# A three-block transformer kernel: another order of work and of loads at the boundaries between its stages

## The chip, the core and the metric

The kernel runs on one core of one Trainium2 chip. A core has a matrix engine (TensorE, here PE; PEld is its loading of weights, which overlaps), a vector engine (VectorE, DVE), an activation engine (ScalarE, ACT), a general one (GpSimd, POOL) and a queue engine that here issues most transfers (SyncE, SP). Every engine works through its own instructions in order and waits for others by semaphores. The metric is the device time of one execution in microseconds (us); smaller is better.

## The reference

The reference is three blocks in a row over x of 512 tokens and 1024 features, all in fp32. Cut to what matters here:

```python
x = first_block(x, ...)    # x + gate1 * mixer(rms(x)), then x + gate2 * conv_ffn(rms(x)), then a last rms norm
x = second_block(x, ...)   # x + gate * (mixed(h) @ w_out), h = rms(x) * (1 + scale) + shift, then a last rms norm
x = third_block(x, ...):
    x = layer_norm(ALPHA * x + 0.5 * swiglu(x), ...)
    x = layer_norm(ALPHA * x + hybrid_mixer(x, mem, ...), ...)
    x = layer_norm(ALPHA * x + 0.5 * swiglu(x), ...)

def layer_norm(x, g, b):
    mu = mean(x); var = mean((x - mu) ** 2)
    return (x - mu) * rsqrt(var + eps) * g + b
```

Each stage thus ends in a product, a residual sum with the old x, and a norm over all 1024 features of a token, and the next stage begins with products of the normed result h. No product of the next stage can be complete before the norm's sum over all features is.

## The kernel before

Features lie on the partitions: x is 8 tiles of 128 features by 512 tokens, and so is h. A product in fp32 is made of three passes: each operand is split into a high part and the rest (`hi` and `lo`), and `dense` (L411) issues for every 128 by 128 weight tile `wh` x `a.hi` (L419), `wh` x `a.lo` (L420) and `wl` x `a.hi` (L422). All 8 (or 22) feature tiles k of the input are added up in one PSUM tile, called `mm` or `sd` after its pool; each pool has four.

Weights come as a stream of chunks of 8 such tiles (`Stream`, L71): a load of 512 KB by SP into one of two staging tiles `wst`, a cast to `whi` on ACT (L102), the rest `wlo` on DVE or POOL (L107). Six chunks have room; `_need` keeps three loaded ahead of the one in use. A chunk's room comes free when the last product with it is done.

`final_stage` (L442) is the end of every stage. The first `nfull` of the 8 output tiles m are made over all 512 tokens, the others in two halves of 256 tokens: first all remaining m of the first half, then all of the second. For every m, `epi` (in `residual`, L613) adds the old x, whose load POOL issues at that moment (L621), and `norm.push` adds to the norm's sums. `norm.finish` makes, for one half, a column sum on PE (L554: a product with a matrix of ones), a root on ACT (L228), a reciprocal on DVE (L229), and then h: per feature tile one `stt` (a scalar_tensor_tensor on DVE, L549), an ACT instruction that writes `hi`, and an `stt` that writes `lo`. It is a generator: the first half's h rows are emitted between the second half's products.

The layer norm (`NormLayer`, L332) subtracts a shift c, got from the first tile, from every x as it is pushed (L343, DVE), adds the x (L347) and their squares (L207), and in `finish` forms mean and variance (L352, L353, an `stt`) and subtracts the mean from 8 tiles, 5 of them on POOL (L357).

`dense_group` (L424) is the beginning of the next stage: a few products (jobs) are made in the first half, one job after the other, each through all 8 features, then all in the second half, with the same weights.

From the end of a first half's norm on, the next 4 chunks have their `wlo` made on POOL (`S.mark`, L485, and `held`), with an order that puts them behind the norm's root and reciprocal.

The program is written in this order, but a scheduler rearranges it for each engine by priorities and free buffers; what an engine then executes in what order is shown below.

The boundaries where this happens, with the numbers used in this document:

1. mixer `w_out` (L1012, rms norm) to `ffn_up` of the first block (L1064): jobs pg and pu for two m, pg in `mm`, pu in `sd`.
2. `w_down` (L1060, two rms norms at once) to `mlstm` of the second block: the gates `if2` (L1157), then q and k products in groups of two (L1231), convolutions over them (L1241), gates on 4 rows (L1159 and further), transposes of the gates (L1163), then v products and the scores (L495).
3. `w_out_2` (L1146, rms norm with a gain) to `ffn_up` of the third block.
4. swiglu's output (L1519, layer norm) to `dsa_index` (L1705): one product for the index keys, three for its queries, transposes of `iwT` (L1733).
5. `w_out_3` (L1547, layer norm) to `ffn_up` of the last swiglu.
6. the last swiglu's output, layer norm, and the kernel's end.

In 2, 4 and 6 the product has 22 feature tiles and `nfull` is 6; in the others it has 8, and `nfull` is 4.

## Time and profile before

| what | value |
|---|---|
| median of 3 runs | 3274.16 us (3274.14 to 3275.22) |
| the profiled execution | 3279.36 us |
| its span, first to last instruction | 3277.6 us |
| mean granted PE clock | 0.988 |
| PE idle in the span | 90 us |

The page's second part cuts the span in 40 slices. Two of its rows:

```profile
PE   8999999999999999999999999999899999989998
DVE  6997676588837756655787353333796747563334
```

Each digit is the busy share of a slice of 82 us in tenths (9 is 90% or more). DVE's row is read in the same way. PE drops below 9 in the first slice, in the slices of boundaries 4 and 5, and at the end; a wait of a few us at a boundary hardly shows at this grain, which is why the windows further down are 20 to 35 us wide. Rows of a timeline give start, length, engine, line, operation, names of output and inputs, form and count, and in brackets the idle time before, with what ended it. POOL's rows:

```profile
L107 POOL TENSOR_TENSOR wlo<-wst,whi 128x1024 fp32r<-128x1024 f32 x20 | 49.9, 2500 | 210.4 <-ACT whi L102 162.8 <-DVE t L549 39.7 <-DVE xh L549 3.6
L357 POOL TENSOR_TENSOR xh<-xh,t 128x256 f32<-128x256 f32 x30 | 26.4, 910 | 122.9 <-ACT t L352 111.8 <-PE sd L554 11.0
```

These are groups of instructions: busy time in all, mean ns of one, idle time before them. POOL made 20 splits (5 boundaries of 4) at 2.50 us each, and 30 subtractions of the mean.

### The profile page before, as it was taken

Reading aid. Unit: us, or ns where it says so; the run is one execution under the profiler, and the core shown is the slowest. Engines: PE = TensorE matmul, PEld = TensorE weight load, DVE = VectorE, ACT = ScalarE, POOL = GpSimd, SP = SyncE. Lnnn points to the kernel's source line nnn. Section 1 sums busy time; section 2 is a strip of 40 time slices with the busy share of each in tenths; the row PEclk is TensorE's granted clock in tenths of the full one; section 3 lists DMA queues with packets and bytes.
Section 4 is the critical chain, followed back from the end, with each engine's and each line's share of the span. In section 5 each row is a group of like instructions: output and inputs, shape, how many; then the busy total and the mean of one; then the engine's idle time right before and its main releaser. Section 6 shows DMA issues by size and latency. Waiting matters only on the chain.

```text
span 3277.6 us, 40053 instructions
## 1 busy us (share of the span) xinstructions
PE 3187.5 (97%) x15534; PEld 2639.8 (81%) x15534; DVE 2035.1 (62%) x3160; ACT 1310.2 (40%) x2010; POOL 193.6 (6%) x268
## 2 busy tenths in 40 slices
PE   8999999999999999999999999999899999989998
PEld 4778788888888888888887888888877787878887
DVE  6997676588837756655787353333796747563334
ACT  4665232344424444333665233222543535342222
POOL 2100000100001000000000010000200012020001
PEclk9999999999999999999999999999999999999999
DMA  5114776423333232222232333333323131333331
GB/s 204 52 58 134 238 223 199 140 90 97 106 113 105 78 90 84 84 90 85 74 97 74 110 116 103 103 106 106 117 75 124 61 105 61 122 103 97 106 109 62
DMA packets 123108, 352.52 MB, mean 108 GB/s; under 512 B 13978, under 2 KB 28668, under 8 KB 122788
## 3 DMA queue, kind: packets, MB, share of 16 engines
q1 hardware_dynamic: 118612, 336.18, 32.6%
q0 software_dynamic: 4304, 13.77, 1.3%
q8 instruction: 122, 2.00, 0.2%
q14 instruction: 70, 0.57, 0.1%
HBM read 337.27 MB, written 16.82 MB: 108 GB/s over the span
## 4 chain that ended last, share of the span: by engine, by line
PE 80%; DVE 11%; DMA 3%; issue 3%; ACT 2%; SPq 0%; POOL 0%; ACTq 0%; DVEq 0%; POOLq 0%
PE mm L420 19%; PE mm L419 19%; PE mm L422 18%; PE sd L420 4%; PE sd L422 4%; PE sd L419 4%; PE mm L440 2%; PE mm L439 2%; PE mm L438 2%; DVE wlo L107 2%; DMA gv<-in_wmod 2%; DVE xh L549 1%; PE sd L495 1%; PE sd L496 1%; PE sd L497 1%
## 5 line engine op out<-in xcount | busy, mean ns | idle before, releaser
L107 DVE TENSOR_TENSOR wlo<-wst,whi 128x1024 fp32r<-128x1024 f32 x496 | 609.4, 1230 | 614.7 <-ACT whi L102 605.5
L102 ACT CAST whi<-wst 128x1024 fp32r<-128x1024 f32 x485 | 509.1, 1051 | 1174.8 <-PE mm L420 732.5
L420 PE MATMUL mm<-xh,whi 128*128 128x512 f32 (+1 forms) x2256 | 857.5, 381 | 16.0 <-DVE xh L549 11.9
L419 PE MATMUL mm<-xh,whi 128*128 128x512 f32 (+1 forms) x2256 | 857.2, 381 | 14.5 <-ACT xh L364 10.5
L422 PE MATMUL mm<-xh,wlo 128*128 128x512 f32 (+1 forms) x2256 | 849.7, 379 | 0.0
L420 PEld LDWEIGHTS mm<-xh,whi 128*128 128x128 f32 x2256 | 430.4, 191 | 94.6 <-DVE xh L549 16.1
L419 PEld LDWEIGHTS mm<-xh,whi 128*128 128x128 f32 x2256 | 429.8, 191 | 94.5 <-ACT xh L364 11.4
L422 PEld LDWEIGHTS mm<-xh,wlo 128*128 128x128 f32 x2256 | 428.3, 191 | 74.0 <-issue 2.9
L419 PE MATMUL sd<-xh,whi 128*128 128x512 f32 (+1 forms) x576 | 215.2, 374 | 0.0
L420 PE MATMUL sd<-xh,whi 128*128 128x512 f32 (+1 forms) x576 | 214.6, 372 | 0.0
L422 PE MATMUL sd<-xh,wlo 128*128 128x512 f32 (+1 forms) x576 | 214.5, 372 | 0.0
L420 PE MATMUL mm<-d,whi 128*128 128x512 f32 (+1 forms) x540 | 187.7, 348 | 0.0
L422 PE MATMUL mm<-d,wlo 128*128 128x512 f32 (+1 forms) x540 | 187.2, 347 | 0.0
L419 PE MATMUL mm<-d,whi 128*128 128x512 f32 (+1 forms) x540 | 187.1, 347 | 0.0
L438 PE MATMUL mm<-whi,xh 128*128 128x512 f32 x336 | 131.7, 394 | 6.1 <-DVE whi L104 3.1
L439 PE MATMUL mm<-wlo,xh 128*128 128x512 f32 x336 | 132.8, 395 | 0.6 <-DVE wlo L107 0.6
L440 PE MATMUL mm<-whi,xh 128*128 128x512 f32 x336 | 132.0, 394 | 0.0
L549 DVE SCALAR_TENSOR_TENSOR t<-t,vec,t 128x441 f32<-128x441 f32 (+2 forms) x176 | 122.7, 701 | 9.6 <-ACT t L1046 5.3
L419 PEld LDWEIGHTS sd<-xh,whi 128*128 128x128 f32 x576 | 109.5, 190 | 18.8
L420 PEld LDWEIGHTS sd<-xh,whi 128*128 128x128 f32 x576 | 109.2, 190 | 18.8
L422 PEld LDWEIGHTS sd<-xh,wlo 128*128 128x128 f32 x576 | 109.2, 190 | 18.7
L1510 DVE TENSOR_TENSOR t<-t,sd 128x512 f32<-128x512 f32 x44 | 30.2, 688 | 144.7 <-PE sd L422 141.1
(482 smaller groups left out, 5187.6 us busy)
## 6 DMA issues: line engine op xcount, KB each, us to landing
wst<-in_w SPq DMA_DIRECT2D x516, 512.0 KB, 3.6
gv<-in_wmod SPq DMA_DIRECT2D x64, 256.0 KB, 3.5
gv<-in_wada SPq DMA_DIRECT2D x48, 256.0 KB, 3.5
t<-xd POOLq DMA_DIRECT2D x40, 256.0 KB, 3.6
xd<-xh SPq DMA_DIRECT2D x72, 128.0 KB, 1.8
wm<-in_wmod SPq DMA_DIRECT2D x32, 256.0 KB, 5.0
tmat<-trow SPq DMA_DIRECT2D x2, 2048.0 KB
tp<-tmat SPq DMA_DIRECT2D x16, 256.0 KB, 2.6
```

Source lines behind the costliest of these rows:

```text
L102: self.after(nc.scalar.copy(hi, st))
L107: self.after(eng.tensor_sub(lo, st, hi.bitcast(FT)))
L419: mm(ps, wh, a.hi[k], start=(k == 0), stop=False)
L420: mm(ps, wh, a.lo[k], start=False, stop=False)
L422: mm(ps, wl, a.hi[k], start=False, stop=(k == K - 1))
L438: mm(ps, a.hi[k][:, s], wh, start=(k == 0), stop=False)
L439: mm(ps, a.hi[k][:, s], wl, start=False, stop=False)
L440: mm(ps, a.lo[k][:, s], wh, start=False, stop=(k == K - 1))
L495: mm(ps, l[0], r[0], start=start, stop=False)
L496: mm(ps, l[0], r[1], start=False, stop=False)
L497: mm(ps, l[1], r[0], start=False, stop=stop)
L549: self.nc.vector.scalar_tensor_tensor(out, in0, s, in1, op0=op0, op1=op1)
```

## The change

It has six parts, all at the boundaries. (A) `dense_group` lets all its jobs step through the features together, and in the second half asks the stream to `fill` chunk rooms that came free; `final_stage` does so too. (B) The order marks and the splits on POOL are taken out: all `wlo` are on DVE. (C) The old x is loaded two tiles ahead, and in the layer norm POOL subtracts the shift from old x (not from tile 0) so that `push` doesn't. (D) In the layer norm's `finish` the square of the mean is made by ACT straight from the column sum, and all 8 subtractions of the mean are on DVE. (E) Two `sd` tiles are set aside ahead of the second half's norm (`spare`) and used by the next stage's first jobs. (F) In `mlstm` the gates' product and the first four q and k products are one group of five jobs, the gates come after it.

```diff
 class Stream:
-        self.after(eng.tensor_sub(lo, st, hi.bitcast(FT)))
-        self.held = max(self.held - 1, 0)
+        nc.vector.tensor_sub(lo, st, hi.bitcast(FT))
...
+    def fill(self, name, k, c0):
+        if not self.recording:
+            end = min(self.at[name, k, c0] + self.RING, (self.i - 1) // CH + 6, (len(self.order) + CH - 1) // CH)
+            while self.loaded < end:
+                self._load(self.loaded)
+                self.loaded += 1
...
 class NormLayer(Norm):
         if m == 0:
             nc.scalar.activation(self.named("c"), self.K.colsum(x), AF.Copy, scale=1.0 / P)
-        nc.vector.tensor_sub(x, x, self.named("c")[:, cols])
+            nc.vector.tensor_sub(x, x, self.named("c"))
...
-        nc.scalar.activation(mu, self.colsum("w", cols), AF.Copy, scale=1.0 / D)
-        nc.vector.tensor_mul(var, mu, mu)
+        sums = self.colsum("w", cols)
+        nc.scalar.activation(var, sums, AF.Square, scale=1.0 / D)
+        nc.scalar.activation(mu, sums, AF.Copy, scale=1.0 / D)
...
-            (nc.gpsimd if k in (2, 4, 5, 6, 7) else nc.vector).tensor_sub(x[k][:, cols], x[k][:, cols], mu)
+            nc.vector.tensor_sub(x[k][:, cols], x[k][:, cols], mu)
...
     def dense_group(self, jobs, a):
-            for ps, name, c0, K in jobs:
-                self.dense(name, c0, K, [(ps[:, cols], v)], again=bool(i))
+            for k in range(KD):
+                for ps, name, c0, K in jobs:
+                    self.dense(name, c0, K, [(ps[:, cols], v)], again=bool(i), ks=range(k, k + 1))
+                if i:
+                    self.S.fill(jobs[0][1], min(k + 1, KD - 1), jobs[0][2])
...
     def final_stage(...):
+                if i:
+                    self.S.fill(name, kfull if m + 1 < KD else K - 1, min(m + 1, KD - 1) * P)
+            if i and norm.h is not None:
+                self.spare = [self.sd() for _ in range(2)]
             rest = norm.finish(cols)
             next(rest)
-            if not i:
-                self.S.mark([act, norm.point], 4)
...
     def residual(self, alloc, scale, shift=None):
+        def load(last):
+            for m in range(len(old), min(last + 1, KD)):
                 old[m] = alloc()
                 self.nc.gpsimd.dma_start(old[m], self.xsrc[m])
         def epi(m, ps, cols):
+            load(m + 2)
+            if shift is not None and m and m not in done:
+                self.nc.gpsimd.tensor_sub(old[m], old[m], shift())
+                done.add(m)
             self.stt(self.x[m][:, cols], ps, scale(m), old[m][:, cols], OP.mult, OP.add)
+        load(1)
...
     def mlstm(...):
+            pgate, first = self.spare[0], [self.spare[1]] + [self.mm() for _ in range(3)]
+            self.dense_group([(pgate, "if2", 0, KD)] + [(first[2 * w + j], "w_in_2", (8 * w + j) * P, KD)
+                                                        for w in range(2) for j in range(2)], h)
```

Lines move by the change: L419, L420 and L422 become L417, L418 and L420; L107 becomes L106, L549 L546, L229 L224, L207 L202, L621 L618. POOL's new subtraction is L623.

**Boundary 1, PE.** The first products of the next stage (first half) before: `mm_5416` is a job, `xh_4900`, `xh_4902`, ... are the `hi` tiles of h for feature 0, 1, ..., and the odd numbers behind them the `lo` tiles.

```order
L419 MATMUL mm_5416<-xh_4900,whi_5112 128x256
L420 MATMUL mm_5416<-xh_4901,whi_5112 128x256
L422 MATMUL mm_5416<-xh_4900,wlo_5114 128x256
L419 MATMUL mm_5416<-xh_4902,whi_5112 128x256
L420 MATMUL mm_5416<-xh_4903,whi_5112 128x256
L422 MATMUL mm_5416<-xh_4902,wlo_5114 128x256
L419 MATMUL mm_5416<-xh_4904,whi_5112 128x256
```

The same place in the changed kernel, where the `hi` tiles are `xh_4904`, `xh_4906`, ...:

```order
L417 MATMUL mm_5430<-xh_4904,whi_5116 128x256
L418 MATMUL mm_5430<-xh_4905,whi_5116 128x256
L420 MATMUL mm_5430<-xh_4904,wlo_5118 128x256
L417 MATMUL mm_5431<-xh_4904,whi_5116 128x256
L418 MATMUL mm_5431<-xh_4905,whi_5116 128x256
L420 MATMUL mm_5431<-xh_4904,wlo_5118 128x256
L417 MATMUL mm_5430<-xh_4906,whi_5116 128x256
```

Before, one job went on to the next feature after three matmuls; now the two `mm` jobs share a feature, so a new one is asked for after six. The two `sd` jobs follow behind the second half's column sum.

**Boundary 1, DVE.** After the first half's reciprocal, in the changed kernel (`s` are norm tiles, `xh_4896` and the like x, `xh_4905` and `xh_4907` the first `lo` tiles of h):

```order
L224 RECIPROCAL s_5223<-s_5223 128x256
L546 SCALAR_TENSOR_TENSOR xh_4896<-mm_5071,gate_735_4888,s_5026 128x256
L106 TENSOR_TENSOR wlo_5190<-wst_5186,whi_5188 128x1024
L546 SCALAR_TENSOR_TENSOR s_5226<-xh_4892,gsf_4890,s_5223 128x256
L546 SCALAR_TENSOR_TENSOR s_5230<-xh_4893,gsf_4890,s_5223 128x256
L546 SCALAR_TENSOR_TENSOR xh_4897<-mm_5072,gate_735_4888,s_5064 128x256
L106 TENSOR_TENSOR wlo_5304<-wst_5300,whi_5302 128x1024
L546 SCALAR_TENSOR_TENSOR xh_4905<-s_5226,mod_115,xh_4904 128x256
L202 TENSOR_TENSOR s_4986<-s_4986,s_5260 128x256
L546 SCALAR_TENSOR_TENSOR xh_4907<-s_5230,mod_115,xh_4906 128x256
```

Before, no split stood between the two halves' reciprocals on DVE; now four do, the first two ahead of the first `lo` tile of h.

**Boundary 5, POOL.** From the first load of old x on, in the changed kernel (`t_22984`, `t_22986`, ... are the tiles of old x, `t_23069` the shift):

```order
L618 DMA t_22984<-xd_0_31_99 128x512
L618 DMA t_22986<-xd_1_32_100 128x512
L618 DMA t_23066<-xd_2_33_101 128x512
L623 TENSOR_TENSOR t_22986<-t_22986,t_23069 128x512
L623 TENSOR_TENSOR t_23066<-t_23066,t_23069 128x512
L618 DMA t_23076<-xd_3_34_102 128x512
L618 DMA t_23116<-xd_4_35_103 128x512
L623 TENSOR_TENSOR t_23076<-t_23076,t_23069 128x512
L623 TENSOR_TENSOR t_23116<-t_23116,t_23069 128x512
L618 DMA t_23155<-xd_5_36_104 128x512
L623 TENSOR_TENSOR t_23155<-t_23155,t_23069 128x512
L618 DMA t_23199<-xd_6_37_105 128x512
```

Before, the eight loads stood here one behind the other with nothing between them. Now loads and subtractions alternate in POOL's one queue, and the issue of load 6 stands behind the subtraction of tile 5, which waits for load 5; tile 7 follows in the same way.

More of the change, by code (lines that the diff above doesn't have):

```diff
@@ L101, in _load @@
         if self.hi_pattern[c % len(self.hi_pattern)] == "a":
[L102 removed]
+            nc.scalar.copy(hi, st)
         else:
[L104 removed]
+            nc.vector.tensor_copy(hi, st)
         lo = pool.tile([P, CH * P], FR, name=f"wlo{c}", tag="wlo", bufs=self.RING)
[L106 to L108 removed]
+        nc.vector.tensor_sub(lo, st, hi.bitcast(FT))
         self.chunks[c] = (hi, lo)
[L111 to L118 removed]
+    def fill(self, name, k, c0):
         if not self.recording:
[L121 removed]
+            end = min(self.at[name, k, c0] + self.RING, (self.i - 1) // CH + 6, (len(self.order) + CH - 1) // CH)
+            while self.loaded < end:
+                self._load(self.loaded)
+                self.loaded += 1
     def prime(self):
@@ L149, in get @@
         self.last[key] = hi[:, j * P:(j + 1) * P], lo[:, j * P:(j + 1) * P]
+        self.at[key] = c
         return self.last[key]
@@ L229, in rsqrt @@
         self.nc.vector.reciprocal(r, r)
-        self.point = self.K.last_of(mybir.EngineType.DVE)
         return r
@@ L337, in __init__, with shift @@
         self.g, self.b, self.h = g, b, h
+    def shift(self):
+        return self.named("c")
     def push(self, m, cols):
@@ L486, in final_stage @@
             norm.post(cols)
-    def last_of(self, engine):
-        if not self.S.recording:
-            return next(i for i in reversed(self.nc.cur_bb.bb.instructions) if i.engine == engine)
     def mm3(self, ps, l, r, start, stop):
@@ L611, in next_x, with residual, epi @@
         self.xi += 1
-    def residual(self, alloc, scale):
+    def residual(self, alloc, scale, shift=None):
         self.new_x()
-        old = {}
-        def epi(m, ps, cols):
-            if m not in old:
+        old, done = {}, set()
+        def load(last):
+            for m in range(len(old), min(last + 1, KD)):
                 old[m] = alloc()
                 self.nc.gpsimd.dma_start(old[m], self.xsrc[m])
+        def epi(m, ps, cols):
+            load(m + 2)
+            if shift is not None and m and m not in done:
+                self.nc.gpsimd.tensor_sub(old[m], old[m], shift())
+                done.add(m)
             self.stt(self.x[m][:, cols], ps, scale(m), old[m][:, cols], OP.mult, OP.add)
+        load(1)
         return epi
@@ L1148, in block2, with mlstm_gates @@
             self.h = h
-    def mlstm_gates(self, h, keep, tmp):
+    def mlstm_gates(self, ps, keep, tmp):
         nc, ai = self.nc, self.ai
@@ L1227, in qk_part @@
                     a = Act()
-                    pss = [self.mm() for _ in range(2)]
-                    jobs = [(pss[j], "w_in_2", (8 * w + 2 * hd + j) * P, KD) for j in range(2)]
-                    if hd == 0:
-                        self.dense_group(jobs, h)
+                    pss = [self.mm() for _ in range(2)] if hd else first[2 * w:2 * w + 2]
                     for j in range(2):
@@ L1515, in swiglu @@
             self.ffn_up(win, tail)
-            epi = self.residual(tt, lambda m: 0.5 / ALPHA)
+            epi = self.residual(tt, lambda m: 0.5 / ALPHA, lambda: norm.shift())
             h = None if last else self.new_h()
@@ L1543, in block3 @@
             tt = lambda: self.t(p, [P, T], "t", bufs=12)
-            epi = self.residual(tt, lambda m: 0.5 / ALPHA)
+            epi = self.residual(tt, lambda m: 0.5 / ALPHA, lambda: norm.shift())
             h = self.new_h()
@@ L1711, in dsa_index @@
             p2 = self.pool("idx", e2)
-            pk = self.mm()
-            pqs = [self.mm() for _ in range(3)]
+            pk = self.spare[0]
+            pqs = [self.spare[1]] + [self.mm() for _ in range(2)]
             self.dense_group([(pk, "ikw", 0, KD)] + [(pqs[m], "w_in_3", 3072 + m * P, KD) for m in range(3)], h)
```

19 lines of the change are left out of this document (3 added, 16 removed).

## The prediction

> **What bounds the kernel now.** I read four views in this order: the page's list of engines, a table of windows around the six places where one stage hands over to the next (numbered 1 to 6 as in the text before), the list of what TensorE waited for, and the timeline inside three of those windows. The page says who is the bound:
> ```profile
> PE 3187.5 (97%) x15534; PEld 2639.8 (81%) x15534; DVE 2035.1 (62%) x3160; ACT 1310.2 (40%) x2010; POOL 193.6 (6%) x268
> L107 DVE TENSOR_TENSOR wlo<-wst,whi 128x1024 fp32r<-128x1024 f32 x496 | 609.4, 1230 | 614.7 <-ACT whi L102 605.5
> t<-xd POOLq DMA_DIRECT2D x40, 256.0 KB, 3.6
> wst<-in_w SPq DMA_DIRECT2D x516, 512.0 KB, 3.6
> ```
> PE is busy 97%, and the change neither adds nor removes a product. All that can be won is idle time of PE, 3277.6 - 3187.5 = 90 us, and matmuls that ran at a lowered clock. The windows show where the boundaries have theirs (columns: window, length, busy time of PE, PEld, DVE, ACT, POOL, granted PE clock, DMA share, GB/s):
> ```profile
> 640.00:660.00 20.00, 15.42 (x100) 14.34 (x100) 18.63 (x30) 7.94 (x18) 7.03 (x3) 0.83 0.32 101
> 1010.00:1040.00 30.00, 24.76 (x177) 23.70 (x176) 27.86 (x48) 13.56 (x28) 7.78 (x3) 0.89 0.32 99
> 1040.00:1062.00 22.00, 20.34 (x141) 19.24 (x140) 19.82 (x41) 10.83 (x18) 5.04 (x11) 0.92 0.48 151
> 1936.00:1956.00 20.00, 16.07 (x100) 15.09 (x99) 17.57 (x26) 7.39 (x15) 7.36 (x3) 0.77 0.49 158
> 2310.00:2340.00 30.00, 24.39 (x171) 22.52 (x171) 28.84 (x48) 17.79 (x39) 14.30 (x13) 0.89 0.48 151
> 2340.00:2360.00 20.00, 17.37 (x134) 16.31 (x133) 13.42 (x21) 13.63 (x27) 4.54 (x5) 0.91 0.48 147
> 2880.00:2915.00 35.00, 24.96 (x170) 23.65 (x171) 31.70 (x55) 19.07 (x43) 15.69 (x13) 0.85 0.30 98
> ```
> I count a window's loss as its idle time plus its busy time times (1 - clock). Boundary 1: (20 - 15.42) + 15.42 x 0.17 = 7.2 us. In the same way boundary 2 has 8.0 + 3.3, boundary 3 7.6, boundary 4 8.3 + 4.2, boundary 5 13.8. The sum, **52 us, is the ceiling** of what the five inner boundaries can give; 19 us of it is clock. DVE is busy for 28 to 32 us of these windows' longest ones, so it is DVE that PE waits for there, as the waits say (us in total, times, longest):
> ```profile
> PE mm L420 <- DVE xh L549: 11.9, 11, 2.9
> PE mm L419 <- ACT xh L364: 10.5, 3, 8.7
> PE mm L420 <- DVE xh L501: 3.7, 2, 2.3
> PE sd L554 <- DVE t L347: 3.5, 3, 1.7
> PE sd L546 <- DVE iwT L1733: 2.6, 1, 2.6
> ```
> These are rows of h (xh), which the next stage's first products need, the sums of the norms (sd at L554), and one wait behind the index stage.
>
> **Stepping through the features together, and the splits off POOL (boundaries 1 and 3).** Inside window 1:
> ```profile
> 647.63 0.39 PE L420 MATMUL mm<-xh,whi 128*128 128x256 f32 x1 [2.87 <-DVE xh L549]
> 647.86 0.28 PE L422 MATMUL mm<-xh,wlo 128*128 128x256 f32 x1
> 647.98 0.28 PE L419 MATMUL mm<-xh,whi 128*128 128x256 f32 x1
> 652.85 0.58 PE L420 MATMUL mm<-xh,whi 128*128 128x256 f32 x1 [1.37 <-DVE xh L549]
> 644.21 2.97 DVE L549 SCALAR_TENSOR_TENSOR s<-xh,gsf,s 128x256 f32<-128x256 f32 x2
> 647.11 0.47 DVE L549 SCALAR_TENSOR_TENSOR xh<-s,mod,xh 128x256 fp32r<-128x256 f32 x1
> 647.50 0.47 DVE L549 SCALAR_TENSOR_TENSOR xh<-mm,gate,s 128x256 f32<-128x256 f32 x1
> 649.08 0.41 DVE L207 TENSOR_TENSOR s<-s,s 128x256 f32<-128x256 f32 x1
> 643.90 2.60 POOL L107 TENSOR_TENSOR wlo<-wst,whi 128x1024 fp32r<-128x1024 f32 x1 [2.15 <-ACT whi L102]
> 2880.00 1.10 PE L554 MATMUL sd<-t,ones 128*128 128x256 f32 x4 [0.35 <-DVE t L347]
> 3267.36 0.51 ACT L228 ACTIVATE t<-t,c 128x256 f32<-128x256 f32 x1 [1.69 <-DVE t L549]
> 2885.87 1.74 DVE L229 RECIPROCAL t<-t 128x256 f32<-128x256 f32 x1
> ```
> A matmul of 256 columns starts 0.12 us after the one before (647.86 to 647.98). DVE starts one such L549 every 0.40 us (647.11 to 647.50), but two took 2.97 us when a split ran on POOL at 643.90: a stall of 2.97 - 0.87 = 2.1 us; POOL made three splits in this window, and I count two such stalls. PE is at a job's third feature by then, since a single job asks for a feature every 3 x 0.12 = 0.36 us, faster than DVE's two L549 per feature (0.80) can serve.
>
> After the change two jobs share a feature: 0.72 us. On DVE the two POOL stalls are gone (4.2 us), but four splits come back between the first half's reciprocal and the end of its h rows. By the new order DVE has 20 L549 (0.40), 3 sums (0.33) and 4 splits (1.14 each in a queue, the 1.23 of the row less its overlap) there: 8.0 + 1.0 + 4.6 = 13.6 us. The first sum of squares now stands 13 matmuls into the second half (1.6 us); with its own 0.55 (two of them 1.10), the root's 0.5, the reciprocal's 1.74 and some 0.5 of hand-overs, DVE starts at 4.9 and ends at 18.5 us. PE finishes its 96 second-half matmuls and the sum at 12.1 and asks for the last feature at 12.1 + 7 x 0.72 = 17.1. So **1.4 us of waiting is left**, and then the two sd jobs (48 x 0.12 = 5.8 us) hide the second half's chain (0.33 + 0.55 + 0.5 + 1.74 + 4 x 0.40 + 0.5 = 5.2). If a row of that cover is late, its lateness is paid in full. Boundary 1 gives 7.2 - 1.4, say 6, and boundary 3, of the same form with four splits too, 6. Bounds: 2 (every split also waits 1 us for its cast) to 7.
>
> **Boundary 2, products before gates.** PE here comes out of the five joint products early and then has little to do:
> ```profile
> 1048.05 0.43 PE L1163 MATMUL sd<-ident,hm 36*128 36x36 f32 x4 [1.66 <-ACT hm L1159]
> 1049.30 0.55 DVE L1241 TENSOR_SCALAR t<-pad,vec 128x512 f32<-128x512 f32 x1
> 1080.15 0.69 DVE L501 TENSOR_TENSOR qk<-t,qk 128x512 fp32r<-128x512 f32 x1
> 1057.55 0.40 PE L438 MATMUL mm<-whi,xh 128*128 128x512 f32 x1
> 1057.79 0.40 PE L439 MATMUL mm<-wlo,xh 128*128 128x512 f32 x1
> 1082.78 0.50 PE L495 MATMUL sd<-qk,qk 128*128 128x512 f32 x1
> ```
> Before, the gates and q were done near 1046 (the matmul before the 1048.05 row's wait), DVE ran the convolutions and gates from 1049.30 to 1080.84 (31.5 us), and PE had the k products (to 1057.5) and v (96 x 0.23 = 22.5 us with a little between) as cover, so that the scores at 1082.78 waited for nothing. After, all five products are done at 1057.5 - 0.4 - 11.3 + 1 = about 1046.8, no earlier than q was. DVE's chain of 31.5 us starts 3 us after that, as before, with the same five splits in it, and ends near 1081. PE has the gate's transpose, with its 1.7 us of waiting, and v: until 1071.3. So **some 10 us of waiting appear in front of the scores, and the 11.3 us saved come back**: the boundary gives 1 us. Bounds: -2 (chain longer by the gate rows that now start later) to +5 (DVE's three idle spots in the chain close, and the gates move ahead).
>
> **Boundaries 4 and 5, layer norms.** At 4 the first part is like 1, 8.3 - 1.6 = 6.7; the index transposes then stand behind all four joint jobs, and their wait (2.6 us, above) grows by what PE reaches them earlier; I charge 1.7. It gives 5, bounds 2 to 8. At 5:
> ```profile
> 2892.87 0.80 PE L419 MATMUL mm<-xh,whi 128*128 128x256 f32 x2 [8.71 <-ACT xh L364]
> 2865.64 0.42 DVE L549 SCALAR_TENSOR_TENSOR xh<-mm,t 128x256 f32<-128x256 f32 x1
> 2877.77 0.75 DVE L549 SCALAR_TENSOR_TENSOR xh<-mm,t 128x256 f32<-128x256 f32 x2
> 2850.41 0.60 ACT L342 ACTIVATE t<-sd 128x512 f32<-128x512 f32 x1
> L1653 POOL TENSOR_TENSOR t<-t,o 128x512 f32<-128x512 f32 x4 | 5.1, 1286 | 174.3 <-ACT t L1650 174.3
> 2883.02 4.19 POOL L357 TENSOR_TENSOR xh<-xh,t 128x256 f32<-128x256 f32 x5
> ```
> The 8.71 us are a sum that came too late: m = 7 of the first half was only added at 2877.77, behind second-half work. After, the sum stands nine matmuls into the second half, but POOL now makes old x minus the shift, in one queue with its loads. The shift is there at 2851.0. A subtraction of 128x512 is not in the trace; the multiplication of that size takes 1.29 us, and by the 128x256 row (4.19 / 5 = 0.84) it would be 1.7; I take 1.3, and 0 to 2.4 (the split of twice the size) as bounds. Subtractions 1 and 2, issues 3 and 4 (about 0.54 each), 3 and 4 landing after 3.6, subtractions 3 and 4: 2860.5. Then each of 5, 6, 7 costs issue 0.5 + landing 3.1 to 3.6 + 1.3, about 4.9: ready at 2865.4, 2870.3, 2875.2. PE's first-half products are there 2.9 us apart (24 x 0.12), m = 4 at about 2862.9 and m = 7 at 2871.5. So the sum waits for POOL until 2875.2 + 1.4 (stt, square, add) = 2876.6, and PE, which gets there at 2872.6, **loses 4 us**, about 2.5 more to the clock after it, 1.3 as at boundary 1: 13.8 - 7.8 = 6. Bounds: 1 (subtractions of 2.4) to 11 (POOL in time).
>
> The Trainium skill, "SBUF — State Buffer", section "Who interferes with whom", says that a VectorE instruction with two SBUF inputs and a GpSimd one that reads SBUF exclude each other for a whole instruction, and that the order of issue decides. The 2.97 us above agree, and the rule speaks against the new subtractions: by it the sums L347 and L207 of three pushes could each stand 1.3 us longer, and boundary 5 would give 6 - 3.9 = 2.
>
> **The end.** The last push loses one subtraction (0.42), the chain one multiplication that waited for it, and gets five subtractions on DVE (5 x 0.33 = 1.7) that partly stand beside the root. I count 0.5 us, bounds -1 to +1.5. The splits back on DVE elsewhere (18 stand between the two reciprocals of the five boundaries, 2 before) cost nothing further, as DVE is at 62%.
>
> **The sum.** 6 + 1 + 6 + 5 + 6 + 0.5 = 24.5 us. The profiled execution took 3279.36 us (1.8 more than its span) and would take 3254.9; the median of the runs, 3274.16, stands 5.2 us below it, so I forecast 3249.7, **3250 us**. What a measurement can tell from no change is about 0.2%, 6.5 us.
>
> The Trainium skill, "TensorE: Matmul & The Clock Gate", Part 1, has the clock fall only after an idle window of about 3.4 us. Here a wait of 1.37 us is followed by a matmul of 0.58 instead of 0.28 us, so the trace does not agree; by the page, the short waits that are left would cost no clock, and the sum would be some 2 us larger.
>
> **Rivals.** (a) *POOL and the gates give most of it back.* POOL's chain slips further (subtractions of 1.7 to 2.4 us that hold up DVE's sums) and boundary 2 loses 2: 6 - 2 + 6 + 2 + 1 - 1 = 12, 3262 us. For it: POOL's row of 0.84 for half the size; against: at 4 and 6 products have 22 tiles, and POOL has time. (b) *Nearly all closes*: loads in time, the chain at 2 shorter than I count: 7 + 5 + 7 + 8 + 11 + 0.5 = 38.5, 3236 us. (c) *Slower: the 18 splits in DVE's queue wait for their casts.* DVE stood idle ahead of a split for 614.7 / 496 = 1.24 us on average, for ACT's cast, and where these 18 stand, h rows are queued behind. With 1.23 us each, which are counted, nothing is lost; if each also waits for a load of 3.6 us, 18 x 3.6 = 65 us are added where nothing covers, of which the two stage buffers hide perhaps a third: 43 - 24.5 = +19, 3293 us. It turns slower when a split waits over 24.5 / 18 = 1.4 us uncovered. Against it: loads run ahead over two buffers, and most of DVE's idle time ahead of splits lies where DVE had no work. (d) *Nothing is won*: the time saved at a boundary comes back as waits later, as I count for 2, at the others too: 3274.
>
> **Chances.** Forecast 0.60 (its own range 3240 to 3258), (a) 0.17, (b) 0.10, (c) 0.06, (d) 0.07. The range that leaves out (c), (d) and the far side of (b) is 3235 to 3265. Faster 0.60 + 0.17 + 0.10 = 0.87, same 0.07, slower 0.06.
>
> **What would show it.** Boundaries 1 and 3: waits for xh under 2 us, no L549 of 1.5 us. Boundary 2: a new wait of 5 to 12 us before the scores. Boundary 5: a wait of 3 to 6 us at the first sum, for an xh that waited for POOL, and none of 8.7. DVE waits of over 1.4 us ahead of splits inside a boundary would make me wrong towards (c).

## The result and the profile after

The changed kernel takes 3239.76 us (median of 4 runs, 3237.26 to 3242.88) against 3274.15 us before: a ratio of 0.9895, 95% interval 0.9878 to 0.9912. It is 34.4 us faster where 24 were forecast. That is inside the range (3235 to 3265), but just under the 3240 to 3258 that the chances gave as the forecast's own, and nearer to the sum of rival (b), 3236, than to 3250. The profiled execution took 3240.74 us with a span of 3239.0 us, 38.6 us less than before; the two gains differ because the profiled execution of before stood 5.2 us above its median and this one only 1.0.

The page's rows of the engines and of the splits:

```profile
PE 3172.6 (98%) x15534; PEld 2626.8 (81%) x15534; DVE 2011.7 (62%) x3175; ACT 1312.0 (41%) x2016; POOL 148.5 (5%) x239
L106 DVE TENSOR_TENSOR wlo<-wst,whi 128x1024 fp32r<-128x1024 f32 x516 | 632.8, 1228 | 608.2 <-ACT whi L102 599.7
```

PE does the same 15534 matmuls and is busy 14.9 us less, so part of the gain is clock (mean granted clock 0.995, before 0.988); its idle time fell from 90 to 66 us. DVE made 20 splits more and is nevertheless busy 23 us less. The windows of the changed kernel at the boundaries (columns as before; a window lies where the one of before lay in the program, as nearly as the shifted times allow):

```profile
632.00:652.00 20.00, 19.19 (x150) 18.18 (x149) 16.59 (x31) 9.77 (x18) 0.00 (x0) 1.00 0.44 138
1002.00:1032.00 30.00, 29.77 (x245) 29.46 (x245) 29.83 (x62) 13.93 (x28) 1.38 (x3) 1.00 0.37 114
1054.00:1075.00 21.00, 17.91 (x80) 13.74 (x79) 19.77 (x41) 11.14 (x23) 0.20 (x2) 0.92 0.30 91
1920.00:1940.00 20.00, 19.37 (x157) 18.91 (x156) 17.81 (x33) 9.74 (x19) 0.00 (x0) 1.00 0.51 158
2288.00:2318.00 30.00, 30.00 (x248) 29.79 (x247) 27.80 (x63) 21.02 (x46) 4.28 (x8) 1.00 0.59 188
2318.00:2340.00 22.00, 19.14 (x143) 15.37 (x142) 18.50 (x32) 17.18 (x35) 0.00 (x0) 1.00 0.46 147
2842.00:2877.00 35.00, 30.97 (x232) 29.79 (x233) 31.48 (x71) 21.00 (x46) 0.00 (x0) 0.95 0.35 109
```

Boundaries 1 and 3 lost 7.2 and 7.6 us and now lose 0.8 and 0.6. Boundary 4's first window has no idle time at all. By this count the windows lost 52 us before and lose 15 now. POOL's column is the other thing that changed: 7.03, 7.36 and 14.30 us of work before, 0, 0 and 4.28 now. What is left is a wait behind boundary 2 (4.5 us by the same count: 3.1 idle, 1.4 clock), short waits in boundary 4's second window (2.9 us, all idle) and boundary 5 (5.6 us; another 1.25 us of idle time lie just ahead of its window).

For a count that doesn't depend on how windows are laid, I divide the timeline of PE at the first matmul of 256 columns of each boundary's output product, that is where the last product of a stage changes from all tokens to halves; that matmul is the same in every kernel. I call the stretch from one such matmul to the next a piece. The lengths of the pieces, each with its boundary at its beginning, in us:

| kernel | 1 | 2 | 3 | 4 | 5 | 6 to the last PE row |
|---|---|---|---|---|---|---|
| before | 362.2 | 937.0 | 363.8 | 577.2 | 369.5 | 35.6 |
| changed | 356.1 | 930.2 | 356.8 | 566.0 | 363.7 | 35.1 |
| gain | 6.1 | 6.8 | 7.0 | 11.2 | 5.8 | 0.5 |
| forecast | 6 | 1 | 6 | 5 | 6 | 0.5 |

The six gains make 37.4; another 1.4 came ahead of boundary 1, where the profiles of all the kernels scatter by 4.6 us (615.8 to 620.5). Four terms are right within 1 us. Boundaries 2 and 4 gave 6 us more each than forecast, beyond the bounds that I had set for them (-2 to 5, 2 to 8).

### The profile page after: what moved, and what is told of

It is laid out like the page before. It is cut to its first block, busy times and chain, and to the rows that moved or that the text cites. A ratio compares the mean times of both kernels' runs of the same rounds, so it can differ in the third digit from the quotient of the medians.

```text
span 3239.0 us, 40002 instructions
## 1 busy us (share of the span) xinstructions
PE 3172.6 (98%) x15534; PEld 2626.8 (81%) x15534; DVE 2011.7 (62%) x3175; ACT 1312.0 (41%) x2016; POOL 148.5 (5%) x239
## 4 chain that ended last, share of the span: by engine, by line
PE 81%; DVE 9%; DMA 3%; issue 3%; ACT 3%; POOL 0%; SPq 0%; ACTq 0%; DVEq 0%; POOLq 0%
PE mm L418 19%; PE mm L417 19%; PE mm L420 19%; PE sd L417 4%; PE sd L420 4%; PE sd L418 4%; PE mm L439 2%; PE mm L441 2%; PE mm L440 2%; DVE wlo L106 2%; DMA wst<-in_w 1%; PE sd L492 1%; PE sd L493 1%; PE sd L494 1%; DMA gv<-in_wmod 1%
## 5 line engine op out<-in xcount | busy, mean ns | idle before, releaser
L106 DVE TENSOR_TENSOR wlo<-wst,whi 128x1024 fp32r<-128x1024 f32 x516 | 632.8, 1228 | 608.2 <-ACT whi L102 599.7
L417 PE MATMUL mm<-xh,whi 128*128 128x512 f32 (+1 forms) x2192 | 833.5, 381 | 4.5 <-ACT xh L362 3.2
L418 PE MATMUL mm<-xh,whi 128*128 128x512 f32 (+1 forms) x2192 | 833.0, 381 | 4.3 <-DVE xh L546 2.5
L420 PE MATMUL mm<-xh,wlo 128*128 128x512 f32 (+1 forms) x2192 | 828.8, 380 | 0.0
L417 PEld LDWEIGHTS mm<-xh,whi 128*128 128x128 f32 x2192 | 413.2, 189 | 82.7 <-ACT xh L362 3.6
L418 PEld LDWEIGHTS mm<-xh,whi 128*128 128x128 f32 x2192 | 413.6, 189 | 80.9 <-DVE xh L546 4.2
L420 PEld LDWEIGHTS mm<-xh,wlo 128*128 128x128 f32 x2192 | 411.7, 189 | 74.7 <-issue 3.3
L417 PE MATMUL sd<-xh,whi 128*128 128x512 f32 (+1 forms) x640 | 232.9, 364 | 0.0
L420 PE MATMUL sd<-xh,wlo 128*128 128x512 f32 (+1 forms) x640 | 232.0, 362 | 0.0
L418 PE MATMUL sd<-xh,whi 128*128 128x512 f32 (+1 forms) x640 | 232.0, 362 | 0.0
L417 PE MATMUL mm<-d,whi 128*128 128x512 f32 (+1 forms) x540 | 187.5, 347 | 0.0
L418 PE MATMUL mm<-d,whi 128*128 128x512 f32 (+1 forms) x540 | 187.3, 347 | 0.0
L420 PE MATMUL mm<-d,wlo 128*128 128x512 f32 (+1 forms) x540 | 187.1, 347 | 0.0
L418 PEld LDWEIGHTS sd<-xh,whi 128*128 128x128 f32 x640 | 120.8, 189 | 18.9
L420 PEld LDWEIGHTS sd<-xh,wlo 128*128 128x128 f32 x640 | 120.7, 189 | 18.8
L417 PEld LDWEIGHTS sd<-xh,whi 128*128 128x128 f32 x640 | 120.7, 189 | 18.7
L546 DVE SCALAR_TENSOR_TENSOR t<-t,vec,t 128x441 f32<-128x441 f32 (+2 forms) x176 | 120.6, 694 | 5.2 <-ACT t L1050 1.3
```

What stands on the lines that cost most here:

```text
L106: nc.vector.tensor_sub(lo, st, hi.bitcast(FT))
L417: mm(ps, wh, a.hi[k], start=(k == 0), stop=False)
L418: mm(ps, wh, a.lo[k], start=False, stop=False)
L420: mm(ps, wl, a.hi[k], start=False, stop=(k == K - 1))
L546: self.nc.vector.scalar_tensor_tensor(out, in0, s, in1, op0=op0, op1=op1)
```

## The experiments

Every kernel of this section was timed against the kernel before on its own chip, and profiled. Two theories stood against each other at first. By **stepping**, the joint steps of part A gave DVE the time it lacked. By **splits**, the four splits on POOL behind every first half had held DVE up, and taking them off (part B) was enough. The forecast had put both in one sum.

**The changed kernel again**, as a measure for the others.

> The changed kernel again, as the measure for the other runs of its chip: 3237 to 3243 us, with the loss at boundaries 1 to 5 (idle time of PE and lowered clock) at about 1, 1, 1, 4 and 6 us.

Measured: 3237.79 us (3237.08 to 3241.23), ratio 0.9887 (0.9872 to 0.9902); pieces 355.8, 930.2, 356.8, 565.4, 364.0, 35.1. Between these two profiles the pieces repeat within 0.6 us, better than the whole times (a spread of 4 to 6 us), so I read most experiments from them; one run below moves a piece by 1.6 us that its edit doesn't touch, so less than 2 us in one piece of one run decides nothing.

**A undone: jobs one after the other** (the `fill` of part A stays).

```diff
-            for k in range(KD):
-                for ps, name, c0, K in jobs:
-                    self.dense(name, c0, K, [(ps[:, cols], v)], again=bool(i), ks=range(k, k + 1))
-                if i:
-                    self.S.fill(jobs[0][1], min(k + 1, KD - 1), jobs[0][2])
+            for n, (ps, name, c0, K) in enumerate(jobs):
+                self.dense(name, c0, K, [(ps[:, cols], v)], again=bool(i))
+                if i:
+                    nx = jobs[min(n + 1, len(jobs) - 1)]
+                    self.S.fill(nx[1], 0 if n + 1 < len(jobs) else KD - 1, nx[2])
```

> Jobs of a first group one after the other again (A undone, prefetch kept). Theory 'stepping': a single job asks for a feature every 0.36 us while DVE needs 0.80, so waits for xh of 2 to 4 us come back at each of boundaries 1, 3, 4 and 5, with a low clock behind them: 12 to 22 us slower than the changed kernel, 3252 to 3262. Rival 'splits': the waits of before came from DVE's stalls beside POOL's splits; these are still gone, so at most 5 us slower, below 3245.

Measured: 3239.54 us, ratio 0.9890 (0.9875 to 0.9905); pieces 356.3, 925.6, 357.2, 566.8, 363.7, 35.1. Stepping is worth nothing here: pieces 1, 3, 4 and 5 stay within 0.8 us of the changed kernel's (within 1.4 of its second profile's), and piece 2 is 4.6 us shorter. At boundary 1 PE waits 0.6 us for a `lo` row of h and 0.3 for a `hi` row, against 0.55 with joint steps, although the same four splits stand in DVE's chain. The first theory fell here.

**B undone: four splits on POOL.**

```diff
-        nc.vector.tensor_sub(lo, st, hi.bitcast(FT))
+        (nc.gpsimd if self.held else nc.vector).tensor_sub(lo, st, hi.bitcast(FT))
+        self.held = max(self.held - 1, 0)
...
             next(rest)
+            if not i and not self.S.recording:
+                self.S.held = 4
```

> The four splits after a first half's norm on POOL again (B undone, without the order marks), the joint stepping kept. Theory 'stepping': DVE loses up to 2.1 us per split to the stall but is spared 1.14 of its own work, and joint jobs leave it 0.72 us a feature: 0 to 6 us slower, 3240 to 3246. Rival 'splits': 10 us or more slower, over 3250, with L546 rows of 1.5 us or more at boundaries 1 and 3 and PE waiting for xh there.

Measured: 3269.78 us, ratio 0.9982 (0.9973 to 0.9991): 32 us slower than the changed kernel, though all other parts are in. Pieces 363.1, 933.9, 363.9, 575.8, 365.4, 35.1. Its timeline at boundary 1 shows how (columns as in the timelines before; POOL, then DVE):

```profile
635.82 2.40 POOL L107 TENSOR_TENSOR wlo<-wst,whi 128x1024 fp32r<-128x1024 f32 x1 [42.60 <-ACT whi L103]
639.18 2.71 POOL L107 TENSOR_TENSOR wlo<-wst,whi 128x1024 fp32r<-128x1024 f32 x1 [0.95 <-ACT whi L103]
...
636.18 2.32 DVE L550 SCALAR_TENSOR_TENSOR xh<-s,mod,xh 128x256 fp32r<-128x256 f32 x1 [0.34 <-ACT xh L237]
...
638.76 0.47 DVE L550 SCALAR_TENSOR_TENSOR xh<-s,mod,xh 128x256 fp32r<-128x256 f32 x1
...
639.56 2.61 DVE L550 SCALAR_TENSOR_TENSOR xh<-s,mod,xh 128x256 fp32r<-128x256 f32 x1
```

Two rows of 0.47 us last 2.32 and 2.61, and each ends 0.28 us after POOL's split (638.50 against 638.22, 642.17 against 641.89). These two splits on POOL, of 2.40 and 2.71 us, take 1.85 and 2.14 us from DVE, where on DVE each would take 1.14. Without the order marks POOL's splits lie elsewhere than before, so this run is not the kernel before with five parts added.

**B alone: the kernel before with its 20 splits on DVE** (its order marks stay).

```diff
-        eng = nc.gpsimd if self.held or self.lo_pattern[c % len(self.lo_pattern)] == "p" else nc.vector
+        eng = nc.gpsimd if self.lo_pattern[c % len(self.lo_pattern)] == "p" else nc.vector
```

> The kernel before with one edit: its 20 splits on POOL are on DVE (B alone, its order marks kept). Theory 'splits': POOL's stalls were most of the loss, so this alone gives 5 to 7 us at boundaries 1 and 3, 3 to 4 at 2, 8 to 10 at 4, 2 to 6 at 5: 20 to 32 us, 3243 to 3255. Rival 'together': splits on DVE without joint stepping and prefetch stand in the way of h rows, and it gives less than 10 us, 3265 or more.

Measured: 3240.55 us (3236.34 to 3240.99), ratio 0.9884 (0.9869 to 0.9899). **One line gives the whole gain**, more than I had expected (3243 to 3255); most of the surplus is at boundary 2, 10.4 us where 3 to 4 were expected. Pieces 354.4, 926.6, 355.6, 569.1, 366.3, 35.6: it beats the changed kernel at boundaries 1, 2 and 3 (by 1.7, 3.6 and 1.2) and loses to it at 4, 5 and 6 (by 3.1, 2.6, 0.5), which makes zero. Its window at boundary 1 has no idle time and a full clock:

```profile
634.00:654.00 20.00, 20.00 (x165) 19.81 (x164) 19.44 (x38) 11.52 (x23) 0.00 (x0) 1.00 0.33 106
```

**A alone: the kernel before with joint steps.**

```diff
-            for ps, name, c0, K in jobs:
-                self.dense(name, c0, K, [(ps[:, cols], v)], again=bool(i))
+            for k in range(KD):
+                for ps, name, c0, K in jobs:
+                    self.dense(name, c0, K, [(ps[:, cols], v)], again=bool(i), ks=range(k, k + 1))
```

> The kernel before with one edit: a first group's jobs step through the features together (A alone, without prefetch); splits stay on POOL. Theory 'splits': DVE's stalls remain and are longer than a joint step's 0.72 us covers: at most 8 us of gain, 3266 to 3276. Rival 'stepping': as the forecast had it, 0.72 us a feature hides what DVE needs: 10 us or more, below 3265.

Measured: 3279.44 us, ratio 1.0011 (1.0001 to 1.0020): no gain, if anything a loss. Its window at boundary 1 and some of its waits for h, sums and queries:

```profile
640.00:660.00 20.00, 14.38 (x91) 13.70 (x90) 17.53 (x31) 7.49 (x16) 4.52 (x2) 0.74 0.20 67
...
PE mm L419 <- ACT xh L364: 8.7, 1, 8.7
...
PE mm L420 <- DVE xh L550: 7.4, 7, 2.2
...
PE mm L419 <- DVE iq L502: 5.0, 1, 5.0
...
PE sd L555 <- DVE s L207: 3.5, 1, 3.5
```

PE waits there as before the change (14.38 us busy against 15.42; the 3.5 us for the sum `s` are in this window), and the 8.7 us at boundary 5 are untouched. The 5.0 us for a query (iq) are new: they stand at boundary 4, whose piece is 581.4 us against 577.2 before.

**The stall by itself: POOL reads, and nothing is waited for.** DVE makes all splits as in the changed kernel; POOL makes a subtraction from the same tiles, into the staging tile that nothing reads any more.

```diff
         nc.vector.tensor_sub(lo, st, hi.bitcast(FT))
+        if self.held:
+            nc.gpsimd.tensor_sub(st, st, hi.bitcast(FT))
+        self.held = max(self.held - 1, 0)
```

with `held` set to 4 as in the run of B undone.

> The changed kernel, DVE makes every split as there; in addition POOL makes a subtraction of 128x1024 from the same two tiles (into the staging tile, which nothing reads any more) for each of the four chunks after a first half's norm. Nothing waits for its result but the next load into that tile. Theory 'stall': POOL's reads of SBUF alone hold up DVE's two-input rows by 2 us each, so boundaries 1 and 3 lose 4 us or more each again, and the sum is 15 to 35 us over the changed kernel. Rival 'late splits': what cost time with splits on POOL was that they were done later (2.5 us instead of 1.2); DVE makes them in time here, so less than 6 us are lost.

Measured: 3273.55 us, ratio 0.9992 (0.9982 to 1.0001): 34 to 36 us over the two medians of the changed kernel, and 35 by the pieces: all of the gain is gone. Pieces 360.0, 935.2, 364.6, 575.3, 372.8, 35.1. The rival (splits that came late) falls: here they come in time, from DVE. The rows at boundary 1:

```profile
637.00 2.56 POOL L109 TENSOR_TENSOR wst<-wst,whi 128x1024 f32<-128x1024 f32 x1 [43.82 <-DVE wlo L107]
...
637.22 2.62 DVE L206 TENSOR_TENSOR s<-s,s 128x256 f32<-128x256 f32 x1
...
644.60 2.81 POOL L109 TENSOR_TENSOR wst<-wst,whi 128x1024 f32<-128x1024 f32 x1 [5.05 <-DVE wlo L107]
...
645.12 2.58 DVE L552 SCALAR_TENSOR_TENSOR xh<-s,mod,xh 128x256 fp32r<-128x256 f32 x1
```

A sum of 0.41 us takes 2.62, and it ends 0.28 us after POOL's subtraction. Of the 20 subtractions, 13 take 2.1 to 2.2 us from one row of DVE, five take 0.7 to 1.9, and two take nothing: 33 us in all. POOL's subtraction writes SBUF too, and the run doesn't separate its reads from its writes. The edit also holds a staging tile some 2.5 us longer, which I did not take apart; but no row of the list of PE's waits names a weight there, and the stalled rows carry the loss.

The means of the same group of DVE rows, h's first step at boundary 1, show it at a glance, in the order before, A alone, B alone, changed (busy us, mean ns of one):

```profile
L549 DVE SCALAR_TENSOR_TENSOR s<-xh,gsf,s 128x256 f32<-128x256 f32 x16 | 13.3, 874 | 0.0
L550 DVE SCALAR_TENSOR_TENSOR s<-xh,gsf,s 128x256 f32<-128x256 f32 x16 | 13.3, 875 | 0.0
L549 DVE SCALAR_TENSOR_TENSOR s<-xh,gsf,s 128x256 f32<-128x256 f32 x16 | 6.9, 479 | 0.0
L546 DVE SCALAR_TENSOR_TENSOR s<-xh,gsf,s 128x256 f32<-128x256 f32 x16 | 6.9, 480 | 0.0
```

**The shift on DVE again** (a part of C undone).

```diff
         if m == 0:
             nc.scalar.activation(self.named("c"), self.K.colsum(x), AF.Copy, scale=1.0 / P)
-            nc.vector.tensor_sub(x, x, self.named("c"))
+        nc.vector.tensor_sub(x, x, self.named("c")[:, cols])
...
-            epi = self.residual(tt, lambda m: 0.5 / ALPHA, lambda: norm.shift())
+            epi = self.residual(tt, lambda m: 0.5 / ALPHA)
```

> The shift subtracted from x on DVE again in every push, old x still loaded two tiles ahead. Theory 'POOL chain': PE's wait of 2.0 us at the first sum of boundary 5 goes, since nothing waits for POOL, and a push costs DVE 0.35 more (128x256) or 0.6 (128x512): within 3 us of the changed kernel, and the wait at the first sum under 0.7 us. Rival 'DVE pays': the wait at the sum stays at 2 us or grows, as it comes from DVE's chain, and the kernel is 2 to 6 us slower.

Measured: 3240.68 us, ratio 0.9890 (0.9874 to 0.9907); pieces 355.9, 930.5, 356.9, 567.3, 361.9, 35.6. At boundary 5 it is 1.8 to 2.1 us better, and the wait for the first sum has left the list; at 4 and at the end it loses as much. The POOL chain is real, and small.

**Old x at its first use again** (the other part of C undone).

```diff
-            load(m + 2)
+            load(m)
...
-        load(1)
```

> Old x loaded at its first use again, POOL's subtraction of the shift kept. Theory 'POOL chain': every tile then costs issue, 3.6 us of landing and 1.3 us in a row on POOL, over 5 us a tile, against 2.9 us of PE a half tile at boundary 5: the first sum there waits 8 us or more instead of 2, and the kernel is 6 to 12 us slower. Rival: loads have time, within 2 us.

Measured: 3242.06 us, ratio 0.9899 (0.9882 to 0.9915); pieces 355.9, 929.9, 356.7, 566.1, 363.9, 35.2. The pieces are those of the changed kernel within 0.3 us, so my theory missed. The loads do come later: POOL's last subtraction at boundary 5 ends 18.0 us after the boundary's first matmul, against 13.5 in the changed kernel. But the first half's sum now stands behind 73 matmuls of the second half instead of 9, so PE has work in the meantime, and its wait moves to the first row of h behind that sum (4.0 us). A longer chain on POOL and a later sum cost nothing here. (The median stands 2 to 4 us higher than those of the changed kernel, its range overlaps them, and the profile shows nothing for it.)

**No `sd` tiles set aside** (E undone).

```diff
-            if i and norm.h is not None:
-                self.spare = [self.sd() for _ in range(2)]
...
-            pk = self.spare[0]
-            pqs = [self.spare[1]] + [self.mm() for _ in range(2)]
+            pk = self.mm()
+            pqs = [self.mm() for _ in range(3)]
```

and in the same way in `ffn_up`; in `mlstm` the two tiles stay `sd` tiles, taken where they are used.

> No sd tiles set aside ahead (E undone); the first jobs take whatever PSUM tile comes free (for boundaries 2 and 4: pk and q in mm). Theory: the first jobs then wait for the mm tiles of the final stage's last tiles, or, at 2 and 4, fewer jobs can start in the first half, so the cover of the second half's chain shrinks: 2 to 6 us slower, mostly at boundary 4 (index wait over 1 us again). Rival: sd tiles are free anyhow: within 1 us.

Measured: 3246.37 us, ratio 0.9912 (0.9897 to 0.9927); only piece 4 moved, 572.7 against 565.4 and 566.0. The wait is not the one I named (`iwT`) but this one:

```profile
PE mm L417 <- DVE iq L496: 5.8, 1, 5.8
```

a product that waits until DVE has split a query (iq). So E is worth 7 us in the changed kernel. The same wait stands in the run of A alone (5.0 us), and neither in the kernel before nor in the runs of B alone and of A undone: in these runs it comes with joint steps that have no tiles set aside, so E mends what A brings.

**Gates first, then q and k** (F undone).

```diff
-            self.dense_group([(pgate, "if2", 0, KD)] + [(first[2 * w + j], "w_in_2", (8 * w + j) * P, KD)
-                                                        for w in range(2) for j in range(2)], h)
+            self.dense_group([(pgate, "if2", 0, KD)], h)
...
+                    if not hd:
+                        self.dense_group([(pss[j], "w_in_2", (8 * w + j) * P, KD) for j in range(2)], h)
```

> In the second block the gates' product alone first, then q, then k products in groups of two, all stepping jointly (F undone). Theory 'early chain': the gain at boundary 2 (6.7 us to the next boundary) comes from five jobs in one step, which give DVE 1.8 us per feature, and from the gates' product being done 1.4 us before the group's end; alone it takes 0.36 us a feature, so 3 to 7 us come back, 3243 to 3247, with PE waiting for xh and for the gates' bias. Rival 'norm only': boundary 2 gained from the norm and the splits alone, and the order of gates and products changes less than 1.5 us.

Measured: 3235.08 us (3232.28 to 3237.89), ratio 0.9876 (0.9861 to 0.9891); piece 2 is 926.0 against 930.2. My theory had the wrong sign: undoing F gains 4 us. The runs of A undone (925.6) and of B alone (926.6), whose jobs come one after the other, have the same 4 us. The difference is where the gates stand. First the copy of the gates on DVE and PE's product with the finished gates (`part`) in this run, then the same two rows of the changed kernel (this run started boundary 1 only 1.5 us sooner):

```profile
1031.75 0.17 DVE L1167 COPY gf<-sd 128x16 f32<-128x16 f32 x1 [0.66 <-PE sd L1165]
1050.04 0.49 PE L1264 MATMUL sd<-part,sel 36*128 36x512 f32 x1
...
1038.63 0.18 DVE L1167 COPY gf<-sd 128x16 f32<-128x16 f32 x1
1064.96 0.47 PE L1263 MATMUL sd<-part,sel 36*128 36x512 f32 x1 [2.12 <-DVE part L1204]
```

With the gates first, their chain on DVE runs while PE still has products to make, and PE doesn't wait for them; in a group of five they come after all of them.

**Subtractions of the mean beside the rows** (a variant of D).

```diff
-        for k in range(KD):
+        for k in range(2):
             nc.vector.tensor_sub(x[k][:, cols], x[k][:, cols], mu)
         yield
         for k in range(KD):
             xk = x[k][:, cols]
+            if k > 1:
+                nc.vector.tensor_sub(xk, xk, mu)
```

> The layer norm's subtractions of the mean for tiles 2 to 7 stand beside each tile's h row instead of all eight ahead of the first. At boundary 5 PE waits 2.8 us for the second half's first h row, and six subtractions (6 x 0.33 = 2.0 us) stand ahead of it on DVE. Theory 'queue': the wait falls by 1.5 to 2 us, 2 to 3 us faster in all with the clock. Rival: the wait is for ACT or the sum, and nothing changes (within 0.7 us in that window).

Measured: 3240.69 us, ratio 0.9895 (0.9880 to 0.9910); piece 5 is 1.0 to 1.3 us shorter, pieces 2 and 4 longer by 1.2 to 1.8, though nothing of piece 2 was edited. Inconclusive in all, too small where it was aimed; and the expectation had misread the wait, which is for the seventh row of h of the first half (shown under boundary 5 below), not for the first of the second half.

**A version from these**: the changed kernel with F undone, and the shift on DVE at boundary 5 alone.

```diff
+        elif not self.early:
+            nc.vector.tensor_sub(x, x, self.named("c")[:, cols])
...
-            epi = self.residual(tt, lambda m: 0.5 / ALPHA, lambda: norm.shift())
+            epi = self.residual(tt, lambda m: 0.5 / ALPHA)
             h = self.new_h()
             norm = NormLayer(self, tt, self.x, "ln2g", "ln2b", h)
+            norm.early = False
```

beside the edit of F undone.

> The changed kernel with the gates' product and q, k in groups of two again (as in the run that undid that part), and with the shift on DVE in the one stage with products of 8 tiles ahead of boundary 5. From the runs that did one of these alone: 4.2 us at boundary 2 and 1.8 to 2.1 at boundary 5, so 6 us under the changed kernel: 3231 to 3235. If the two gains of one run each are chance, 3236 to 3241.

Measured: 3233.55 us (3231.03 to 3236.55), ratio 0.9867 (0.9851 to 0.9884); pieces 355.8, 926.1, 356.9, 565.3, 360.7, 35.1. It has the lowest median of the study; its range overlaps that of F undone. Against the changed kernel the two gains are plain in the pieces (4.1 us at boundary 2, 3.0 at 5); the intervals of the two whole times still overlap.

## Why the prediction came out as it did

The whole came out inside the range and its main reason was not what happened. Of the signs named ahead, those for boundaries 1 and 3 came, and the 8.7 us at boundary 5 went; the wait of 5 to 12 us at boundary 2 (3.1) and the one of 3 to 6 us at boundary 5's first sum (2.0) did not come. Step by step:

**What bounds the kernel.** Right: PE waited for DVE at the boundaries, and the 52 us counted in the windows were the ceiling; 37.4 of the 38.6 us that the span lost lie in the six pieces. What made DVE late were its stalls beside POOL's splits, at all five boundaries: B alone gains 7.8, 10.4, 8.2, 8.1 and 3.2 us there.

**Boundaries 1 and 3: the size was right, the credit wrong.** I wrote that PE "asks for a feature every 0.36 us, faster than DVE's two L549 per feature (0.80) can serve", and let the joint step's 0.72 close that. This step failed: it compares two rates as if both engines started together. DVE has the second half's 96 matmuls as a lead, and without stalls the h rows are done, or within 0.6 us of it, when PE arrives, in whatever order the jobs come (A undone shows it with four splits in the chain, B alone with one). In the run of B alone, with jobs one after the other, these are the reciprocal and the last `lo` row of the first half:

```profile
636.08 1.75 DVE L229 RECIPROCAL s<-s 128x256 f32<-128x256 f32 x1
...
647.24 0.48 DVE L549 SCALAR_TENSOR_TENSOR xh<-s,mod,xh 128x256 fp32r<-128x256 f32 x1
```

9.9 us from the end of the one to the end of the other, against the 11.5 that I gave PE's second half. The stalls, which I had priced (2.1 us each), were the loss: without them B alone gains 7.8 and 8.2 us here, as much as the windows had lost. What I had called a cost of B, four splits of 1.14 in DVE's chain, is real but covered: 0.55 us of waiting are left at boundary 1 where I had 1.4.

The rule of the Trainium skill, "SBUF — State Buffer", section "Who interferes with whom", that VectorE with two SBUF inputs and a GpSimd instruction reading SBUF exclude each other for a whole instruction, is borne out by every stalled row above: each starts after POOL's instruction and ends 0.3 us behind it. I had weighed it only against POOL's new subtractions; its weight lay on the splits that were removed. The subtractions do stall DVE (the L340 rows of 128x512 take 1056 ns in the changed kernel and 690 with the shift on DVE) but where nobody waits:

```profile
L340 DVE TENSOR_TENSOR xh<-xh,t 128x512 f32<-128x512 f32 x3 | 3.2, 1056 | 3.7 <-ACT t L339 3.7
...
L340 DVE TENSOR_TENSOR xh<-xh,t 128x512 f32<-128x512 f32 x16 | 10.8, 690 | 2.7 <-ACT t L339 2.3
```

(The first row is of the changed kernel, the second of the run with the shift on DVE.)

**Boundary 2: forecast 1, measured 6.8.** The failing step is "DVE's chain of 31.5 us starts 3 us after that, as before", and with it the 10 us of waiting in front of the scores. In the changed kernel:

```profile
1038.15 0.55 DVE L1243 TENSOR_SCALAR t<-pad,vec 128x512 f32<-128x512 f32 x1 [2.88 <-ACT pad L1241]
1066.89 0.68 DVE L498 TENSOR_TENSOR qk<-t,qk 128x512 fp32r<-128x512 f32 x1
1066.40 0.46 PE L1265 MATMUL sd<-part,sel 36*128 36x512 f32 x1 [0.97 <-DVE part L1204]
```

The chain starts with the group's end (PE's last product of it starts at 1038.0), not 3 us later, because the gates' job and the first q are first in every step and ACT could copy them while PE finished the others; it is 29.4 us long, and PE waits 2.12 us (the row shown with F undone) and 0.97, 3.1 in all, not 10. I was right that F's order costs something here: 4 us, by the three runs without it. The gain itself came from the splits: B alone gives 10.4 us at this boundary, and the changed kernel keeps 6.8 of them.

**Boundary 4: forecast 5, measured 11.2.** I charged 1.6 of waiting at the first products and 1.7 for a longer index wait. The first is not there (30.00 of 30 us busy), and the index wait became shorter instead, 0.53 us where 2.6 stood. B alone gives 8.1 of the 11.2. The `sd` tiles, which I had not priced, are worth 7 in the changed kernel, against a wait that joint steps bring.

**Boundary 5: 6 and 5.8, and that the two agree is luck.** The step that failed is "The 8.71 us are a sum that came too late". The first half's sum stands behind 70 matmuls of the second half in the kernel before and behind 69 in the run of B alone, and yet PE waits 3.03 us there. From the sum's start to PE's first product with h it is 12.9 us before and 7.2 in B alone. The difference is three stalls of DVE behind that sum, beside POOL's splits, 5.7 us together; the rows of the kernel before, and behind the three dots the same rows of DVE and PE's wait in the run of B alone:

```profile
2880.65 2.40 POOL L107 TENSOR_TENSOR wlo<-wst,whi 128x1024 fp32r<-128x1024 f32 x1 [18.77 <-ACT whi L102]
2887.18 4.82 POOL L107 TENSOR_TENSOR wlo<-wst,whi 128x1024 fp32r<-128x1024 f32 x2
2881.19 2.15 DVE L353 TENSOR_TENSOR t<-t 128x256 f32<-128x256 f32 x1 [1.00 <-ACT t L352]
2887.53 2.27 DVE L207 TENSOR_TENSOR t<-t,t 128x256 f32<-128x256 f32 x1
2889.72 3.74 DVE L549 SCALAR_TENSOR_TENSOR xh<-xh,vec,t 128x256 f32<-128x256 f32 x4
...
2846.20 0.43 DVE L353 TENSOR_TENSOR t<-t 128x256 f32<-128x256 f32 x1 [0.99 <-ACT t L352]
2850.88 0.35 DVE L207 TENSOR_TENSOR t<-t,t 128x256 f32<-128x256 f32 x1
2851.15 1.26 DVE L549 SCALAR_TENSOR_TENSOR xh<-xh,vec,t 128x256 f32<-128x256 f32 x3
2852.21 0.51 PE L419 MATMUL mm<-xh,whi 128*128 128x256 f32 x2 [3.03 <-ACT xh L364]
```

Of the 5.8 us B alone gives 3.2. An early sum is not the rest: with old x loaded at its first use the sum comes as late as before, and the piece is as short as in the changed kernel (363.9 and 363.7). Which part gives the other 2.6 us stays open; the subtractions of the mean, moved from POOL to DVE in part D, were not undone in any run. POOL's chain is as I had it: a subtraction takes 1.3 us and a tile 4.5 (4.9 forecast), and DVE waits for it.

```profile
2835.92 1.29 POOL L623 TENSOR_TENSOR t<-t,t 128x512 f32<-128x512 f32 x1 [2.62 <-DMA t<-xd]
2840.45 1.26 POOL L623 TENSOR_TENSOR t<-t,t 128x512 f32<-128x512 f32 x1 [2.73 <-DMA t<-xd]
2841.74 0.43 DVE L546 SCALAR_TENSOR_TENSOR xh<-mm,t 128x256 f32<-128x256 f32 x1 [3.10 <-POOL t L623]
2842.77 1.12 PE L551 MATMUL sd<-t,ones 128*128 128x256 f32 x4 [2.02 <-DVE t L344]
2860.83 1.04 ACT L102 CAST whi<-wst 128x1024 fp32r<-128x1024 f32 x1 [1.50 <-DMA wst<-in_w]
2862.33 0.80 PE L417 MATMUL mm<-xh,whi 128*128 128x256 f32 x2 [2.76 <-ACT xh L362]
```

PE waits 2.0 us at the first sum (4 forecast) and, which I had not seen, 2.76 for the seventh of the first half's eight rows of h: that row starts on ACT at 2861.78, behind a cast of weights that had waited 1.50 us for its load.

**The end** gave 0.5, as forecast. **Rival (c)**, splits that wait in DVE's queue, did not happen: between the two halves' reciprocals a split waits 0.27 us at most at boundary 1, and none waits over 0.8 at the others.

**The clock.** The prediction set the 1.37 us wait at boundary 1 ahead of the slow matmul behind it. The clock was lowered before that wait: it is 1.00 from 646.00 to 649.50 and 0.50 from 649.70 to 651.40, where PE is busy all the time; the wait that goes ahead of it is the one of 2.87 us. The short waits that are left still cost clock: the 2.12 and 0.97 us at boundary 2, which lie close together, and the 2.76 at boundary 5 are followed by some 3 us at 0.50 (1066.80 to 1070.10, 2862.20 to 2865.50).

**From span to median.** I took the 5.2 us between the profiled execution and the median of before over to the changed kernel, where they are 1.0. This hid 4 of the 14 us by which the terms fell short, so that the forecast missed by 10; that the two errors partly cancel is luck too.

## What to carry to other kernels

Work given to an idle engine is free only if it takes nothing from the busy one. Look for rows of the busy engine that last several times their usual length and end when the idle engine's row ends, before moving work between the two. When several parts change at once, a run of each part alone is worth more than a sum: here one line gives as much as all six parts, joint steps give nothing, the five joint jobs cost 4 us, one part mends what another brings, and one was not taken apart. Before comparing two engines' rates, ask how much lead the slower one has.
